# Three of four pooling groups by a seven-product scheme, with block sums made by adding DMAs

## The chip, the cores and the metric

One core of one Trainium2 chip runs the whole program as one launch. The metric is the device time of that launch in microseconds (us). TensorE is PE, VectorE is DVE, ScalarE is ACT, GpSimd is POOL, and SyncE is SP, which issues most DMAs.

## The reference, cut to what matters

Two layers run over 512 latent and 256 context tokens of width 1024. The first has four mLSTM heads beside four pooling groups. The second is windowed attention and is not touched. For a pooling group, with 256 channels, the reference computes two projections of the normalized stream h (768 tokens by 1024 features), the value u and the gate g, and then

```python
ug = u.astype(f32).reshape(bsz, n, P_GROUPS, P_GROUP_DIM)          # P_WINDOWS = (2, 4, 8, 16)
...
mean = win_sum / (hi - lo).astype(f32)[None, :, :, None]
mixed = jnp.einsum('bngc,gcd->bngd', mean - ug, pool_w.astype(f32))
return mixed.reshape(bsz, n, P_WIDTH) * pool_scale                 # then times silu(gate), then w_out
```

## The kernel before

Every fp32 product is made of three passes with high and low halves: weights and stream are split into a high half (cast on ACT) and a low half (subtraction on DVE, some on POOL), and PE adds high by high, high by low and low by high in PSUM.

The stream is kept transposed as hhi and hlo, eight tiles each of 128 features by 768 tokens. `dense_units` (L229) walks the list `chunks0` (L207) and yields the matmuls of the projections; a chunk is one projection of 256 channels, its weights come in four tiles of 256 KB. In the heads these matmuls fill the gaps of the recurrence; `side_work` puts pieces of other work between them (products of the time embedding on DVE, tiles `mjk`, L719). The chunk u of one pooling group already runs as filler in the last head; its matmuls (`acc_u`) and those of the transposes `ytp` (L918) end the head.

Then comes the pool stage. For a group, u and g are two halves m of 128 channels; a half is 48 matmuls, in turn with 512 and 256 columns (L260), three passes over eight feature tiles. `evict_u` (L949) copies the half from PSUM on ACT into a padded row `up`, adds windows on DVE (L961), multiplies by a table of reciprocal counts and subtracts (L964, L965), and splits the result into dh and dl. `evict_g` (L973) takes tanh on ACT and multiplies on DVE (L976). `mix` (L981) multiplies dh and dl by the group's 256 x 256 weights, 12 matmuls for a half, scales on DVE (L992) and stores the half (L993) into `ysp`. The mix of a group runs in the middle of the next group's u. PSUM accumulators of these projections come from `pacc` (L175), which has two buffers: a third must wait until the first is evicted.

The output projection (`po`, L1090) takes 16 such stored blocks with their weights `ows`; its first blocks are loaded ahead, behind marks of the pool stage (`MARK`, `MARKD`, L1073), and split on ACT (`owh`, `oyh`) and DVE (`owl`, `oyl`).

A Tile scheduler turns the text into one instruction queue for each engine, in program order, with semaphores; each engine takes its queue in order. POOL computes the scale of each head (`rs_hd`, `rr_hd`, L148, L150), which DVE needs at the end of that head (L909), and little else there.

Of the kernel before, what the change touches and what calls it, by code (L numbers as in the profile page):

```python
# [10 lines left out]
F32 = mybir.dt.float32  # L11
# [60 lines left out]
MARK = (3, 0)  # L72
# [7 lines left out]
MARKD = (2, 0)  # L80
SN = (1, 1, 1, 1)
SK = 3.0
# [25 lines left out]
def tile_trunk(ctx: ExitStack, tc: tile.TileContext, x, c, ctx_in, c_ctx, w_mod, b_mod, g_pre, g_post,  # L108
               w_in, b_gate, conv_w, mnorm, pool_w, pool_scale, w_out, c_w_in, c_sink, c_w_out,
               w_mod_t, w_mod_0, win_c, cwin_c, vecs, inv_cnt, cos_t, sin_t, out):  # L110
# [48 lines left out]
    ps2 = cst.tile([P, KT], F32, name="ps2")  # L159
    kcw = cst.tile([P, 48], F32, name="kcw")  # L160
# [49 lines left out]
    chunks0 += [(k_, g) for g in range(4) for k_ in "ug"]  # L210
# [88 lines left out]
    with ExitStack() as st0:  # L299
# [163 lines left out]
        V.tensor_scalar(ps2, cv[:, CPS:CPS + KT], 0.5, None, op0=ALU.mult)  # L463
        V.tensor_copy(kcw, cv[:, CCV:CCV + 48])
# [81 lines left out]
    ysp = [dram.tile([P, T], F32, name=f"ysp{i}") for i in range(16)]  # L546

    with ExitStack() as sth:
# [178 lines left out]
        def gate_half(l, w, n, ops):  # L727
# [4 lines left out]
            def item(k):  # L732
                wst = mp.tile([P, 512], F32, tag="wmt", name=f"wmg{nm}{k}", bufs=WB)
                SY.dma_start(wst, w_mod[l][k * P:(k + 1) * P, cols])
                yield
                if k == 0:
                    acc.append(mp.tile([P, 512], F32, tag="macc", name="macc" + nm, bufs=1))
                    G.memset(acc[0], 0.0)
                    SY.dma_start(acc[0][0:1, :], b_mod[l:l + 1, cols])
                ko(V.scalar_tensor_tensor(acc[0], wst, cs[:, w, k:k + 1], acc[0], op0=ALU.mult, op1=ALU.add))  # L740
# [28 lines left out]
        for h in range(H):  # L769
# [101 lines left out]
            def side_n(i):  # L871
                for _ in range(SN[i]):
                    side_work()

# [32 lines left out]
            r2 = rstd_from(ssq, 4 * DH, NT, gp, "hd")  # L907
            for t in range(NT):
                V.scalar_tensor_tensor(hs[:, t, :], hs[:, t, :], r2[:, t:t + 1], zz[:, t, :],  # L909
                                       op0=ALU.mult, op1=ALU.mult)  # L910
# [12 lines left out]
        while side or begun:  # L923
            side_work()


    with ExitStack() as stp:
        pp = stp.enter_context(tc.tile_pool(name="pool", bufs=2, reuse_waits="tile"))
        ups = []
        W_P = PAD + NX + PAD + NC + PAD  # L930
        WU = NX + PAD + NC
        for i in range(2):
            up = pp.tile([P, W_P], F32, name=f"up{i}", bufs=1)
            G.memset(up, 0.0)
            ups.append(up)

        cst_g, dd, zg = {}, {}, {}

        def pool_consts(g):
            ivt = pp.tile([P, WU], F32, tag="ivt", name=f"ivt{g}", bufs=1)  # L940
            SY.dma_start(ivt, inv_cnt[g:g + 1, :].to_broadcast([P, WU]))
            pws = pp.tile([P, 2, DH], F32, tag="pws", name=f"pws{g}", bufs=1)
            SY.dma_start(pws, pool_w[0, g].rearrange("(k p) c -> p k c", p=P))
            pwh = pp.tile([P, 2, DH], F32R, tag="pwh", name=f"pwh{g}")
# [655 lines left out]
```

## Time and profile before

| what | us |
|---|---|
| device time, median of 3 runs | 1094.92 (1093.55 to 1096.0) |
| device time of the profiled execution | 1093.02 |
| its span | 1091.1 |
| PE busy in the span | 1062.9 (97%) |
| DVE busy | 741.6 (68%) |
| ACT busy | 529.0 (48%) |
| POOL busy | 116.9 (11%) |

The time of a run is a little more than the span that the profiler shows, because the span begins and ends with the first and last instruction of an engine. Busy shares are of the whole span; what a stage is bound by is read from that stage.

### The profile page before, as it was taken

To read this page: it belongs to the slowest core of one execution; us is meant where nothing else is said; L and a number is where in the kernel's file an instruction comes from. 1 tells how busy PE (TensorE), PEld (TensorE's weight loads), DVE (VectorE), ACT (ScalarE), POOL (GpSimd) and SP (SyncE) were. 2 spreads that over 40 slices of the span, in tenths; PEclk is the share of its full clock that TensorE was granted. 3 is DMA by queue.
4 is the path that set the end of the run, shared out by engine and by line. 5 is a ranking of instruction groups with operands and counts; after the bars stand their busy time and mean duration, and the time that the engine had idled before them with its cause. 6 is when DMAs were issued, how large, how long until landed. Compare 5 with 4: busy or idle time off the path is not lost.

```text
span 1091.1 us, 18584 instructions
## 1 busy us (share of the span) xinstructions
PE 1062.9 (97%) x7071; PEld 959.4 (88%) x7071; DVE 741.6 (68%) x1638; ACT 529.0 (48%) x1025; POOL 116.9 (11%) x154
## 2 busy tenths in 40 slices
PE   8999999999999999999999999999999999999997
PEld 4898999999989998998888888878899999998875
DVE  4975775767677767778656455576574777777776
ACT  5953533344344433533232225465474666667772
POOL 2100000000000000001000000110015223214211
PEclk9999999999999999999999999999999999999999
DMA  8543352435333434334332348766213111103103
GB/s 341 166 146 88 102 142 73 140 107 134 95 121 114 119 101 132 101 103 126 112 117 82 111 140 276 231 209 237 72 40 90 57 40 57 50 21 97 40 20 116
DMA packets 66881, 127.26 MB, mean 117 GB/s; under 512 B 9884, under 2 KB 21340, under 8 KB 66792
## 3 DMA queue, kind: packets, MB, share of 16 engines
q1 hardware_dynamic: 66792, 126.08, 36.7%
q8 instruction: 55, 0.90, 0.3%
q14 instruction: 34, 0.28, 0.1%
HBM read 115.53 MB, written 10.52 MB: 116 GB/s over the span
## 4 chain that ended last, share of the span: by engine, by line
PE 84%; DVE 6%; issue 3%; ACT 3%; DMA 2%; POOL 1%; DVEq 0%; SPq 0%; POOLq 0%; ACTq 0%
PE po L1090 10%; PE acc_v L254 6%; PE acc_g L260 6%; PE acc_u L260 6%; PE acc_z L254 6%; PE acc_k L260 6%; PE acc_o L254 5%; PE acc_q L260 5%; PE acc1z L1368 4%; PE acc1q L1368 4%; PE ph L865 4%; PE pq L817 3%; PE pv L1300 2%; PE S L1262 2%; PE pt L1290 2%
## 5 line engine op out<-in xcount | busy, mean ns | idle before, releaser
L1090 PE MATMUL po<-owh,oyh 128*128 128x512 f32 x192 | 59.6, 391 | 1.2 <-DVE ytp L992 1.2
L1090 PE MATMUL po<-owl,oyh 128*128 128x512 f32 x192 | 59.7, 392 | 0.9 <-DVE owl L141 0.9
L136 ACT CAST ph<-pt 128x512 fp32r<-128x512 f32 x72 | 41.9, 584 | 36.5 <-PE pt L1290 35.9
L1090 PE MATMUL po<-owh,oyl 128*128 128x512 f32 x192 | 59.2, 389 | 0.0
L1277 ACT ACTIVATE p<-p,mx 128x512 f32<-128x512 f32 (+1 forms) x64 | 49.9, 780 | 12.7 <-DVE mx L1275 11.6
L254 PE MATMUL acc_v<-whi_v,hhi 128*128 128x256 f32 (+1 forms) x192 | 55.9, 291 | 0.0
L254 PE MATMUL acc_z<-whi_z,hhi 128*128 128x256 f32 x192 | 55.5, 289 | 0.0
L254 PE MATMUL acc_o<-whi_o,hhi 128*128 128x256 f32 x192 | 54.9, 286 | 0.0
L141 DVE TENSOR_TENSOR pl<-pt,ph 128x512 fp32r<-128x512 f32 x72 | 49.4, 688 | 7.5 <-ACT ph L136 7.0
L254 PE MATMUL acc_v<-whi_v,hlo 128*128 128x256 f32 (+1 forms) x192 | 54.3, 283 | 0.0
L254 PE MATMUL acc_v<-wlo_v,hhi 128*128 128x256 f32 (+1 forms) x192 | 54.2, 282 | 0.0
L254 PE MATMUL acc_z<-whi_z,hlo 128*128 128x256 f32 x192 | 53.9, 281 | 0.0
L254 PE MATMUL acc_o<-whi_o,hlo 128*128 128x256 f32 x192 | 53.8, 280 | 0.0
L254 PE MATMUL acc_o<-wlo_o,hhi 128*128 128x256 f32 x192 | 53.8, 280 | 0.0
L254 PE MATMUL acc_z<-wlo_z,hhi 128*128 128x256 f32 x192 | 53.7, 280 | 0.0
L141 DVE TENSOR_TENSOR owl<-ows,owh 128x1024 fp32r<-128x1024 f32 x32 | 39.1, 1222 | 14.0 <-ACT owh L136 14.0
L1411 PE MATMUL fin<-woh,ohl 128*128 128x512 f32 x128 | 47.7, 413 | 0.7 <-DVE ya L1418 0.7
L1273 DVE CUSTOM_DVE_ANT_0 p<-S,mA,nsk 128x512 f32<-128x512 f32 x48 | 35.9, 747 | 16.3 <-PE S L1262 15.8
L1090 PEld LDWEIGHTS po<-owl,oyh 128*128 128x128 f32 x192 | 35.7, 188 | 9.9 <-DVE owl L141 2.7
L719 DVE SCALAR_TENSOR_TENSOR mjk<-wmt,csb 128x512 f32<-128x512 f32 x64 | 43.7, 684 | 0.3
L1090 PEld LDWEIGHTS po<-owh,oyh 128*128 128x128 f32 x192 | 35.7, 188 | 8.8 <-issue 1.5
L1290 PE MATMUL pt<-ident,p 128*128 128x128 f32 x288 | 43.3, 273 | 0.1
(388 smaller groups left out, 3542.5 us busy)
## 6 DMA issues: line engine op xcount, KB each, us to landing
ows<-in_ab_w_out_dram SPq DMA_DIRECT2D x32, 512.0 KB, 5.4
wmg<-in_w_mod_dram SPq DMA_DIRECT2D x48, 256.0 KB, 2.7
wmod<-in_w_mod_dram SPq DMA_DIRECT2D x16, 512.0 KB, 6.7
wmt<-in_w_mod_t_dram SPq DMA_DIRECT2D x32, 256.0 KB, 3.2
oys<-ysp SPq DMA_DIRECT2D x32, 192.0 KB, 3.1
ws_q<-in_win_c_dram SPq DMA_DIRECT2D x16, 256.0 KB, 2.6
ws_v<-in_win_c_dram SPq DMA_DIRECT2D x16, 256.0 KB
ws_k<-in_win_c_dram SPq DMA_DIRECT2D x16, 256.0 KB, 2.6
```

The source lines that it names most:

```text
L136: S.copy(hi, src)
L141: (lo_eng or V).tensor_tensor(lo, src, f32(hi), op=ALU.subtract)
L254: ko(PE.matmul(acc[:, j, 0:cols], hx[k][:, ts_], ww[k // 2][:, k % 2, 0:cols], start=(k == 0 and i == 0), stop=(k == KT - 1 and i == 2)))
L260: ko(PE.matmul(acc[:, a:b], ww[k // 2][:, k % 2, sl], hx[k][:, a:b], start=(k == 0 and i == 0), stop=(k == KT - 1 and i == 2)))
L719: ko(V.scalar_tensor_tensor(jk, wst, 1.0, csb[:, w_, hf * 512:hf * 512 + 512], op0=ALU.mult, op1=ALU.mult, accum_out=md[:, which, kt, hf, ...
L865: ko(PE.matmul(ph[:, 0:DH], ss[:, s, :], vv[:, s, :], start=(j == 0 and i == 0), stop=(j == len(stl) - 1 and i == 2)))
L1090: ko(PE.matmul(accs[j][:, ns], yy[:, j * P:(j + 1) * P], ww[:, ns], start=(k == 0 and i == 0), stop=(k == 15 and i == 2)))
L1273: V.tensor_tensor_reduce(p_[:, 0:512], pS, mask[:, 0:512], -0.125, sk, ALU.add, ALU.min, mx)
L1277: S.activation(p_[:, 0:n], p_[:, 0:n], AF.Exp, scale=-1.0, bias=mx, accum_out=self.den[:, hh:hh + 1])
L1290: ko(PE.transpose(tp[:, hh * P:(hh + 1) * P], self.ps[hh][:, j * P:(j + 1) * P], ident))
L1368: ko(PE.matmul(acc[:, j, :], hx[t0 + j][:, k, :], ww[k // 2][:, k % 2, :], start=(k == 0 and i == 0), stop=(k == KT - 1 and i == 2)))
L1411: ko(PE.matmul(acc, ohl[:, x_, k, :], ww[4 * b + k][:, ns], start=(k == 0 and pi == 0), stop=(k == 3 and pi == 2)))
```

## The change

Group 1 is computed as before, u in the last head and g first in the pool stage. Groups 3, 2 and 0 are computed by Strassen's scheme in Winograd's form: for a group, u and g (two halves of output channels), two halves of the 1024 features and two halves of the 768 tokens make a 2 x 2 by 2 x 2 block product, which takes seven block products of 256 channels by 512 features by 384 tokens in place of eight. A block product is 24 matmuls, 12 for each half m of 128 channels (four feature tiles, three passes), with 384 columns each (L1144). Three accumulators (y and x from `pacc`, z from `pmisc`) hold partial results that ACT copies out between products and DVE adds.

The scheme needs sums of blocks of h and of the weights. Those of the weights (12 tiles of 512 KB in DRAM) are made by a plain DMA and an adding DMA, both on POOL's queue (`keep_w`, `add_w`). The stream is first put together from its halves in DRAM, in the same way (`keep_h`, `add_h`). That is 40 DMAs of 384 or 512 KB; `sum_step` issues up to 12 in each head. At the end of the last head four blocks of the stream (`raw`, 768 KB each) are loaded back, added and subtracted on DVE (`diff`), cast on ACT (`high`), and the low halves are made on DVE (one) and POOL (three) (`low`).

The windows run over both halves of a group at once (2 x 791 elements), and the reciprocal counts are applied at the edges only. The mixes of one group are put into the products of the next. The first block of the output projection has its own buffers, loaded early; the second waits for the marks.

```diff
+    def keep_h(k):
+        ko(G.dma_start(hdr[k], f32(hhi[k])))
+    def add_h(k):
+        ko(G.dma_start(hdr[k], f32(hlo[k]), accum_op=ALU.add))
+    def keep_w(key, src):
+        ko(G.dma_start(wsum[key], src))
+    def add_w(key, src):
+        ko(G.dma_start(wsum[key], src, accum_op=ALU.add, max_dma_last_dim=8192))
...
             def side_n(i):
...
+                if i != 1 and n < 4:
+                    sum_step()
...
+        raws = {n: hs_p.tile([P, 4, TH], F32, tag="sum", name=f"raw{n}", bufs=5) for n in "6752"}
+        for n, (kk, tt) in zip("7562", ((0, 0), (0, 1), (1, 1), (1, 0))):
+            SY.dma_start(raws[n], hdr[4 * kk:4 * kk + 4, :, TH * tt:TH * tt + TH].rearrange("k p t -> p k t"))
...
+        def high(n):
+            highs[n] = hi_p.tile([P, 4, TH], F32R, name=f"high{n}")
+            with tc.issue_after(zg["u"]):
+                S.copy(highs[n], raws[n])
+        def low(n):
+            lows[n] = hs_p.tile([P, 4, TH], F32R, tag="sum", name=f"low{n}", bufs=5)
+            (G if n in "752" else V).tensor_tensor(lows[n], raws[n], f32(highs[n]), op=ALU.subtract)
...
-        def mix(g):
+        def mix(g, m):
...
+            if g == PAIRS[-1]:
...
+                S.copy(mixed, acc[:, 0:T])
+                acc = mixed
...
+        USES = "1265743"
+        def product(acc, g, n, start, ms=(0, 1)):
+            x_ = operand(n)
+            for m in ms:
+                for k in range(4):
+                    if k == 1:
+                        load_w()
+                    if k == 3:
+                        step()
+                    hi, lo = ready_w[g, n, k // 2]
+                    xh, xl = x_(k)
+                    for i, (ww, hx) in enumerate(((hi, xh), (hi, xl), (lo, xh))):
+                        ko(PE.matmul(acc[:, m, 0:TH], ww[:, k % 2, m * P:(m + 1) * P], hx, ...
+        def pair(g, before):
+            y, z = two(new_acc(f"y{g}")), two(pmisc.tile([P, 1024], F32, tag="qk", name=f"z{g}"))
+            product(y, g, "1", True)
+            ko(S.copy(p1, y[:, :, 0:TH]))
+            product(z, g, "2", True)
+            ko(V.tensor_tensor(up[:, :, PAD:PAD + TH], z[:, :, 0:TH], p1, op=ALU.add))
+            product(y, g, "6", False)
...
+            product(x_, g, "5", True, (0,))
+            product(y, g, "7", False)
...
+            mix(before, 0)
+            product(y, g, "4", False)
...
+            product(x_, g, "5", True, (1,))
...
+            mix(before, 1)
+            product(x_, g, "3", False)
...
+            b = V.tensor_tensor(gx[:, :, L], x_[:, :, 0:TH], gx[:, :, L], op=ALU.add)
+            if last:
+                marks["b"] = b.ins
...
+                    if gi == 0 and k == 0:
+                        ws, ys = first
```

The change moves instructions at places that the diff does not show. The first is DVE where the pool stage opens, from the windows of the first group to the gate's first half `zg`, whose instruction sets an accumulator free (`raw`, `win`, `df`, `dl` are rows of the pool stage, `pwl` and `wlo` low halves of weights). Before, the last head's scale `hs3` stands ahead of it; then:

```order
L961 TENSOR_TENSOR win000_6161<-up0_6147 128x791
L964 TENSOR_TENSOR df00_6163<-win000_6161,ivt0_6151 128x776
L965 TENSOR_TENSOR df00_6163<-df00_6163,up0_6147 128x776
L141 TENSOR_TENSOR pwl0_6156<-pws0_6153,pwh0_6155 128x512
L961 TENSOR_TENSOR win010_6172<-up1_6149 128x791
L141 TENSOR_TENSOR dl00_6167<-df00_6163,dh00_6166 128x776
L964 TENSOR_TENSOR df01_6174<-win010_6172,ivt0_6151 128x776
L965 TENSOR_TENSOR df01_6174<-df01_6174,up1_6149 128x776
L141 TENSOR_TENSOR pwl1_6333<-pws1_6330,pwh1_6332 128x512
L141 TENSOR_TENSOR dl01_6178<-df01_6174,dh01_6177 128x776
L976 SCALAR_TENSOR_TENSOR zg00_6242<-zg00_6242,acc_g00_6193 128x768
```

In the changed kernel the same stretch, behind the four `raw` instructions, reads

```order
L140 TENSOR_TENSOR wlo_311_6341<-ws_311_6339,whi_311_6340 128x2x256
L1043 TENSOR_TENSOR win10_6351<-up_6228 128x2x791
L1031 TENSOR_TENSOR low6_6329<-raw6_6216,high6_6327 128x1536
L140 TENSOR_TENSOR pwl1_6368<-pws1_6226,pwh1_6367 128x512
L1043 TENSOR_TENSOR win11_6401<-win10_6351 128x2x789
L1048 TENSOR_TENSOR win11_6401<-win11_6401,ivt1_6224 128x2x8
L1048 TENSOR_TENSOR win11_6401<-win11_6401,ivt1_6224 128x2x24
L1048 TENSOR_TENSOR win11_6401<-win11_6401,ivt1_6224 128x2x8
L1050 SCALAR_TENSOR_TENSOR win11_6401<-win11_6401,up_6228 128x2x776
L140 TENSOR_TENSOR pwl3_6378<-pws3_6375,pwh3_6377 128x512
L1074 SCALAR_TENSOR_TENSOR zg1_6285<-zg1_6285,acc_g10_6234 128x768
```

The windows of both halves and the edges now stand ahead of the first gate half in longer instructions, with the low half of one block of the stream between them.

The second is DVE a little ahead of it, at the end of the last head (`hs3` is the head's output, `ot3` its squares, `wlo_g` a low half of a gate weight). Before:

```order
L903 SCALAR_TENSOR_TENSOR hs3_5180<-ot3_5349,hs3_5180 128x1536
L905 SCALAR_TENSOR_TENSOR ot3_5349,ssqh_1151<-hs3_5180 128x256 x6
L909 SCALAR_TENSOR_TENSOR hs3_5180<-hs3_5180,rr_hd_5990,zt3_5766 128x256 x6
L141 TENSOR_TENSOR wlo_g02_6038<-ws_g02_6036,whi_g02_6037 128x2x256
L141 TENSOR_TENSOR wlo_g03_6056<-ws_g03_6054,whi_g03_6055 128x2x256
```

and now:

```order
L946 SCALAR_TENSOR_TENSOR hs3_5252<-ot3_5427,hs3_5252 128x1536
L948 SCALAR_TENSOR_TENSOR ot3_5427,ssqh_1166<-hs3_5252 128x256 x6
L140 TENSOR_TENSOR wlo_g12_6114<-ws_g12_6112,whi_g12_6113 128x2x256
L140 TENSOR_TENSOR wlo_g13_6132<-ws_g13_6130,whi_g13_6131 128x2x256
L955 SCALAR_TENSOR_TENSOR hs3_5252<-hs3_5252,rr_hd3_6066,zt3_5839 128x256 x6
```

Two weight halves that stood behind the scaling of `hs3` by `rr_hd` now stand ahead of it.

The third is POOL, from the end of the heads to the first work behind the pool stage. Before:

```order
L738 MEMSET macc101_5439 128x512
L148 TENSOR_SCALAR rs_hd_5988<-ssqh_1151 128x6
L150 TENSOR_TENSOR rr_hd_5990<-rs_hd_5988,mhalf_67 128x6
L934 MEMSET up0_6147 128x792
L934 MEMSET up1_6149 128x792
L141 TENSOR_TENSOR wlo_q00_8549<-ws_q00_8547,whi_q00_8548 128x512
```

and now:

```order
L568 DMA wsum02_750<-wsum05_749 16x8192
L571 DMA wsum02_750<-in_win_c_dram 64x2048
L568 DMA wsum04_751<-wsum02_750 16x8192
L571 DMA wsum04_751<-in_win_c_dram 64x2048
L951 TENSOR_SCALAR rs_hd3_6064<-ssqh_1166 128x6
L953 TENSOR_TENSOR rr_hd3_6066<-rs_hd3_6064,mhalf_67 128x6
L1010 MEMSET up_6228 128x1584
L1031 TENSOR_TENSOR low7_6448<-raw7_6217,high7_6331 128x1536
L1031 TENSOR_TENSOR low5_6470<-raw5_6218,high5_6468 128x1536
L1031 TENSOR_TENSOR low2_6493<-raw2_6219,high2_6491 128x1536
```

The last four DMAs of the block sums stand in head 3, and three low halves of the stream (1536 elements for each partition) come in where POOL had nothing to do.

The fourth is ACT at the start of the output projection (`owh`, `oyh` are its operands, `whi_k` a later weight). Before:

```order
L136 CAST oyh00_7333<-oys00_7329 128x384
L136 CAST owh00_7331<-ows00_7327 128x1024
L136 CAST oyh01_7363<-oys01_7359 128x384
L136 CAST owh01_7361<-ows01_7357 128x1024
L975 ACTIVATE zg31_7242<-acc_g31_7193 128x768
L136 CAST whi_k0_8063<-ws_k0_8062 128x512
L136 CAST whi_k1_8069<-ws_k1_8068 128x512
```

and now:

```order
L1057 CAST dh0_7334<-win00_7284 128x1552
L135 CAST oyh00_7430<-oys00_6203 128x384
L135 CAST owh00_7428<-ows00_6202 128x1024
L1201 ACTIVATE zg0_7339<-gx0_7044 128x1536
L1093 COPY mixed_7355<-acc_mix00_7342 128x768
L135 CAST whi_k0_8160<-ws_k0_8159 128x512
L135 CAST owh01_7458<-ows01_7454 128x1024
L1093 COPY mixed_7355<-acc_mix01_7359 128x768
L135 CAST oyh01_7460<-oys01_7456 128x384
```

The copy of the last mix's second half stands behind the cast `owh01`, whose load waits for the marks.

## Rows read from the trace of the kernel before

**Rows 1.** The page: busy time of the engines over the span (busy us, share, instructions).

```profile
PE 1062.9 (97%) x7071; PEld 959.4 (88%) x7071; DVE 741.6 (68%) x1638; ACT 529.0 (48%) x1025; POOL 116.9 (11%) x154
```

**Rows 2.** Stretches of the span with the busy time of each engine in them (us from the start of the span; busy us and number of instructions for each engine, then the granted TensorE clock, the share of the DMA engines and GB/s). The four are the end of the gates with the first head's opening, the rest of the first head, the pool stage, and the first 30 us of the output projection.

```profile
100.00:125.00 25.00, 22.82 (x188) 22.25 (x187) 16.29 (x50) 13.36 (x31) 0.00 (x0) 1.00 0.34 99
125.00:235.00 110.00, 110.00 (x811) 103.87 (x810) 78.76 (x198) 45.45 (x90) 2.97 (x4) 1.00 0.39 117
514.00:650.00 136.00, 134.85 (x768) 117.62 (x768) 81.13 (x105) 38.17 (x63) 0.00 (x0) 1.00 0.35 112
650.00:680.00 30.00, 29.72 (x130) 24.36 (x131) 15.56 (x20) 12.80 (x19) 0.25 (x1) 1.00 0.83 273
```

**Rows 3.** The chain of work that ended last, through the pool stage (start us, length us, what; x is the number of matmuls). Pieces left out repeat the pattern with the other groups.

```profile
512.27 0.61 ACT whi_u L136
...
513.73 0.28 ACT up L952
...
514.06 17.08 PE acc_g L260 x96
531.14 8.40 PE acc_u L260 x48
539.54 4.20 PE acc_mix L988 x24
...
644.64 4.28 PE acc_mix L988 x24
...
648.95 1.03 DVE ytp L992
...
650.11 12.51 PE po L1090 x54
```

**Rows 4.** The same chain in a head: a run of matmuls with 256 columns each.

```profile
118.30 4.25 PE acc_o L254 x36
```

**Rows 5.** The same chain in the output projection: a run of matmuls with 512 columns each.

```profile
752.16 16.39 PE po L1090 x72
```

**Rows 6.** DVE instruction by instruction at the end of the last head (start us, length us, instruction, in brackets the idle time before it and what ended it).

```profile
505.08 2.46 DVE L909 SCALAR_TENSOR_TENSOR hs<-hs,rr_hd,zt 128x256 f32<-128x256 f32 x6 [2.15 <-POOL rr_hd L150]
507.47 1.28 DVE L141 TENSOR_TENSOR wlo_g<-ws_g,whi_g 128x512 fp32r<-128x512 f32 x2
508.67 0.68 DVE L719 SCALAR_TENSOR_TENSOR mjk<-wmt,csb 128x512 f32<-128x512 f32 x1
...
509.39 0.69 DVE L719 SCALAR_TENSOR_TENSOR mjk<-wmt,csb 128x512 f32<-128x512 f32 x1
```

**Rows 7.** ACT at the same place.

```profile
506.65 0.62 ACT L136 CAST whi_g<-ws_g 128x512 fp32r<-128x512 f32 x1 [1.49 <-PE acc_u L260]
```

**Rows 8.** Groups of DVE instructions by form over the whole run (busy us, mean ns of one, idle time of DVE before them). From the top: 768 elements with one operand in PSUM, 1536 elements with both in SBUF.

```profile
L976 DVE SCALAR_TENSOR_TENSOR zg<-zg,acc_g 128x768 f32<-128x768 f32 x8 | 7.6, 953 | 8.2 <-ACT zg L975 8.1
...
L903 DVE SCALAR_TENSOR_TENSOR hs<-ot,hs 128x1536 f32<-128x1536 f32 x4 | 7.0, 1757 | 8.8 <-ACT hs L867 8.8
```

**Rows 9.** Groups of POOL instructions by form over the whole run, same columns.

```profile
L141 POOL TENSOR_TENSOR wol<-wos,woh 128x512 fp32r<-128x512 f32 x16 | 20.8, 1316 | 23.8 <-issue 14.0 <-ACT woh L136 9.9
L1321 POOL TENSOR_TENSOR og<-gt,ot 128x256 f32<-128x256 f32 x12 | 8.9, 738 | 54.4 <-DVE ot L1320 44.0 <-ACT p L1277 10.3
```

**Rows 10.** POOL instruction by instruction at one place of the output projection.

```profile
679.75 2.56 POOL L141 TENSOR_TENSOR wlo_q<-ws_q,whi_q 128x512 fp32r<-128x512 f32 x2 [173.30 <-ACT whi_q L136]
...
685.22 1.30 POOL L141 TENSOR_TENSOR wlo_q<-ws_q,whi_q 128x512 fp32r<-128x512 f32 x1 [0.22 <-ACT whi_q L136]
```

**Rows 11.** DVE there.

```profile
676.34 0.55 DVE L141 TENSOR_TENSOR oyl<-oys,oyh 128x384 fp32r<-128x384 f32 x1
...
681.32 1.40 DVE L141 TENSOR_TENSOR oyl<-oys,oyh 128x384 fp32r<-128x384 f32 x1 [1.82 <-ACT oyh L136]
...
685.59 1.35 DVE L141 TENSOR_TENSOR oyl<-oys,oyh 128x384 fp32r<-128x384 f32 x1 [1.74 <-ACT oyh L136]
```

**Rows 12.** POOL instruction by instruction at one place near the end of the run.

```profile
1053.84 1.28 POOL L141 TENSOR_TENSOR wol<-wos,woh 128x512 fp32r<-128x512 f32 x1 [2.12 <-ACT woh L136]
```

**Rows 13.** DVE there.

```profile
1053.90 1.25 DVE L1282 TENSOR_TENSOR es<-mx,snk 128x4 f32<-128x4 f32 x1
```

**Rows 14.** One tile of DVE over the whole run: duration ns min/median/max.

```profile
L1282 DVE TENSOR_TENSOR es<-mx,snk x16: 149/156/1246, 846.2 to 1053.9; 128x4 f32<-128x4 f32 x16
```

**Rows 15.** The chain of work in the first head's opening.

```profile
98.93 9.46 DMA qb<-qdr
...
109.32 0.84 ACT kh L136
...
110.19 0.97 DVE kl L141
...
111.20 0.50 PE pq L817 x2
```

**Rows 16.** POOL's instructions in the heads.

```profile
82.09 0.22 POOL L631 COPY pad<-lf 128x48 f32<-128x48 f32 x1 [2.10 <-DVE lf L629]
...
178.22 0.58 POOL L148 TENSOR_SCALAR rs_hd<-ssqh 128x6 f32<-128x6 f32 x1 [18.72 <-DVE ot L905]
...
288.76 0.51 POOL L148 TENSOR_SCALAR rs_hd<-ssqh 128x6 f32<-128x6 f32 x1 [5.45 <-DVE ot L905]
```

**Rows 17.** DMA issues, from the page and from the stretch 630 to 660 us: KB each, median us from issue to landing.

```profile
ows<-in_ab_w_out_dram SPq DMA_DIRECT2D x32, 512.0 KB, 5.4
...
wmod<-in_w_mod_dram SPq DMA_DIRECT2D x16, 512.0 KB, 6.7
...
ysp<-ytp SPq DMA_DIRECT2D x2, 384.0 KB, 2.3
```

**Rows 18.** DVE in the first head, 125 to 235 us: the groups of tensor_scalar.

```profile
L838 DVE TENSOR_SCALAR eb<-ef,rd 128x128 f32<-128x128 f32 (+2 forms) x4 | 1.3, 337 | 0.1
...
L166 DVE TENSOR_SCALAR A<-md,b,cv 128x2 f32<-128x2 f32 x2 | 0.6, 284 | 0.0
```

**Rows 19.** ACT, a group over the whole run: the cast of an output-projection weight.

```profile
L136 ACT CAST owh<-ows 128x1024 fp32r<-128x1024 f32 x32 | 33.6, 1051 | 5.0 <-DMA ows<-in_ab_w_out_dram 5.0
```

More of the change, by code (lines that the diff above doesn't have):

```diff
@@ L922, in tile_trunk @@
                 upto("k", h + 1, side_work)
[L923 to L924 removed]
+        with tc.issue_after(tail["v"]):
+            while side or begun:
+                side_work()
+        while sums:
+            sum_step()
+    ops = ExitStack()
+    op0 = ops.enter_context(tc.tile_pool(name="op0", bufs=1, side="right", reuse_waits="tile"))
+    first = op0.tile([P, D], F32, name="ows00"), op0.tile([P, 384], F32, name="oys00")
     with ExitStack() as stp:
[L928 removed]
@@ L997, in tile_trunk @@
-        pool_consts(0)
-        evict0.update(u=evict_u, g=evict_g)
-        for g in range(4):
-            upto("g", g)
-            if g < 3:
-                pool_consts(g + 1)
-        mix(3)
+            else:
+                acc = pmisc.tile([P, 1024], F32, tag="qk", name=f"mix{g}{m}")
+            for k in range(2):
+                for i, (ww, dx) in enumerate(((pwh, 0), (pwh, 1), (pwl, 0))):
+                    for a, e_, o_ in ((0, NX, 0), (NX, T, PAD)):
+                        ko(PE.matmul(acc[:, a:e_], ww[:, k, m * P:(m + 1) * P], dd[g][dx][:, k, a + o_:e_ + o_],
+                                     start=(k == 0 and i == 0), stop=(k == 1 and i == 2)))
@@ new lines, in tile_trunk, with opening @@
+        evict0.update(u=evict_u, g=evict_g)
+        def opening():
+            for n in "7562":
+                diff(n)
+                yield
+            high("6")
+            low("6")
+            high("7")
+            yield
+            yield from win_steps(FIRST_G)
+            low("7")
+            yield
+            for n in "52":
+                high(n)
+                low(n)
+                yield
+        todo.append(opening())
+        n = 0
+        while ("g", FIRST_G) not in done0:
+            if next(stream0, None) is None:
+                break
+            n += 1
+            if n > 4 and n % 2:
+                step()
+            if n >= SWN and n % 2 == 0:
+                load_w()
@@ L1004, in tile_trunk @@
+        list(consts)
+        SY.dma_start(first[0], w_out[0, 0:P, :])
+        SY.dma_start(first[1], ysp[0][:, 0:384])
+        list(pool_consts(PAIRS[0]))
+        prior = FIRST_G
+        for g in PAIRS:
+            pair(g, prior)
+            prior = g
+        while todo:
+            step()
+        mix(prior, 0)
+        mix(prior, 1)
     l0.close()
```

241 lines of the change are left out of this document (182 added, 59 removed).

## The prediction

> **What bounds the kernel now.** The busy times come first: PE works 97% of the span [rows 1]. The stretches show where: PE is busy 134.85 of 136 us in the pool stage and all of 110 us in a head, at a granted clock of 1.00, while DVE has 55 us to spare in the one and 31 in the other [rows 2]. The chain of waits then names what ends each piece of the pool stage: runs of matmuls one behind the other, and two short breaks, 1.8 us while ACT copies the last u (512.27 to 514.06) and 1.2 us before the output projection [rows 3]. So a matmul saved in the pool stage is worth its whole time, as long as the other engines keep up.
>
> **What the products save.** A group's u and g are 192 matmuls. Runs of 96 and 48 of them take 16.82 and 8.40 us [rows 3], 175 ns each, so 33.6 us a group. The seven products are 168 matmuls with 384 columns, which no row shows. A run of 36 with 256 columns takes 4.25 us [rows 4], 118 ns each, and 72 with 512 columns 16.39 us [rows 5], 228 ns. Halfway is 173 ns; the alternation of both kinds in u and g gives 175. With 173 to 175 a group costs 29.0 to 29.4 us. The saving is 4.2 to 4.6 us a group, over three groups 12.6 to 13.8. I take **-13.2**. The mixes stay 24 matmuls a group, 4.2 us [rows 3].
>
> **The opening of the pool stage** is the largest cost. PE's first product needs an accumulator, and both are held by the gate of group 1 until DVE has done the first `zg`. By the order, that instruction stands behind everything that prepares the sums and the windows.
>
> I add up DVE from the end of the head. Before, the scaling of `hs` ran from 505.08 to 507.5, with two weight halves behind it [rows 6]. Now these stand ahead, and the second waits for its cast, which ended at 507.27 [rows 7]. With 0.64 for that half and 2.46 for `hs`, DVE is free at 510.4, 2.9 us later than before. Then come four `mjk` at a spacing of 0.72 (508.67 to 509.39) [rows 6], 2.9; four `raw` of 1536 elements at 1.76 [rows 8], 7.0; two weight halves 1.3 and small pieces 0.6; the first window, 1582 elements, 1.8; the low half of a block, 1.76. This is 525.8. Two `pwl`, a window, three edges and the difference add 5.4, and `zg` itself 0.95 [rows 8]: 532.1. PE asks for the accumulator at 514.06 + 16.82 = 530.9 [rows 3]. So far 1.2 us late.
>
> But from 525.8 on POOL makes three low halves of 1536 elements. POOL took 0.738 us for 256 and 1.316 for 512 [rows 9], so 3.6 us each by extension, 10.8 in all. And the trace shows what DVE does beside such work. An `oyl` of 0.55 us took 1.40 when it came at 681.32, in the middle of POOL's subtractions, and 1.35 at 685.59, where POOL's ran until 686.52 [rows 10, 11]. At 1053.90 an addition of four elements took 1.25 us and ended just when POOL's instruction of 1.28 us did [rows 12, 13]; its median is 156 ns [rows 14]. All these have both operands in SBUF, and so have the two `pwl`, the window, the edges and the difference.
>
> The bounds are these. If a POOL instruction holds DVE only for as long as a row shows, 1.3 us, three of them cost 3.9 and the first product is 5.1 late. If each holds it to its own end, it is 12.0 late. The rows are nearest to the second, since each hold ended with POOL's instruction; but DVE gets a turn between two, and the durations added up overlap by some 0.07 us each. I take **+8.5**; nothing at all is possible only if POOL comes later than DVE's whole row.
>
> The Trainium skill, "SBUF — State Buffer", section "Who interferes with whom", says that a DVE instruction with two SBUF inputs contends with a GpSimd instruction that reads SBUF, and that the one that comes second blocks fully until the other is done. By that rule the term is the upper bound, 12.0, and my sum comes out 3.5 us longer; the trace agrees for instructions of up to 1.3 us, and none here is longer.
>
> **Smaller terms.** The later `hs` also feeds PE's transposes at the head's end; PE has 48 matmuls of u to put between. Between 0 and the 2.9 us above, I take **+0.8**.
>
> The 12 DMAs that POOL issues from 82 us on [rows 16] meet the load of `qb`, 768 KB, which took 9.46 us and ends a wait of PE (98.93 to 111.20) [rows 15]; that stretch has 2.2 us of PE idle in 25 [rows 2]. Shared between two queues the load could take twice as long, +9.5, or be untouched. The adding DMAs come one after the other, each behind its plain one, so they leave gaps: **+0.6**.
>
> Between the pairs, each has 14 weight tiles to split where a group had 8; 18 more at 0.64 are 12 us of DVE [rows 6], and the opening's 9 us come on top. DVE's 81 us in the stage [rows 2] become some 105 of 123, so a late split now and then: 0 to 3, I take **+0.8**. The load itself rises from 112 GB/s to below 200, where 273 have been moved [rows 2].
>
> The output projection started 1.2 us after the last mix, behind `ytp` of 1.03 us [rows 3]. Now PE's first `po` waits for ACT's copy of the last half mix, which by the order stands behind the cast `owh01`. That weight is loaded only when the last addition on DVE is done, some 1.3 us after the last product. The load takes between 2.3 and 5.4 us by the rows for 384 and 512 KB [rows 17], the cast 1.05 [rows 19] and the copy about 0.8: PE starts 5.5 to 8.6 us after the last product, with 4.2 us of mix in between, so after a break of 1.3 to 4.4 instead of 1.2. I take **+2.0**.
>
> At nothing I cost the windows of the later pairs and the sums in DRAM of the later heads: DVE's spare time and the 61% of the DMA engines' time that is free in a head [rows 2] cover them. If that cover goes, the scaling of the next head's output is late (second rival).
>
> Sum: -13.2 + 8.5 + 0.8 + 0.6 + 0.8 + 2.0 = **-0.5 us**. Against the profiled execution's 1093.02 that is 1092.5; the runs' median is 1.9 higher, 1094.92, which gives **1094.4**.
>
> **The rivals.** *The opening keeps up.* POOL's low halves fall behind DVE's row, or DVE takes its turns first; the stall is 0 to 3 us and PE keeps the saving: 1094.9 - 13.2 + 1.5 + 4.2 = 1087.4, or 1081.7 when the small terms and the stall vanish. For it: the low halves are needed only some 12 us into the pair, and POOL's start hangs on ACT's casts. Against it: each hold in rows 10 to 14. Chance 0.27.
>
> *The blocks of the stream come late* (slower). Four loads of 768 KB in pieces of 1.5 KB must land before DVE can begin; the last is wanted at about 520. If SP issues them at about 500 (an estimate from where the head's tiles come free, rows 6), 273 GB/s [rows 2] lands 3.1 MB in 11.5 us, but the rate of `qb` [rows 15] needs 38. From below some 150 GB/s on, every microsecond later is one of PE: up to 17 more, 1111. Chance 0.09.
>
> *POOL's DMAs are slow* (slower). POOL takes its queue in order, and `rs_hd` of head 0 stands behind 12 of them. From 82.1 to 178.2 [rows 16] there are 96 us, 8.0 for each. The rows for 384 to 512 KB, 2.3 to 6.7 [rows 17], fit; 9.46 would not, and cost 17 us in head 0 and 5 in the next (288.76 less 180.2 is 108.6), 1117. Chance 0.07. The Trainium skill, "SBUF — State Buffer", section "SBUF: two separate sides", warns that a DMA issued from GpSimd waits for its descriptors while DVE runs an instruction in a two-port mode; copies, casts and tensor_scalar are of that kind. In a head of 110 us DVE has 1.9 us of tensor_scalar [rows 18], so by that rule the rival gains nothing.
>
> *The matmul with 384 columns costs as much as two with 256.* Then 168 cost 236 ns each and the saving turns into a loss of 18 us; even at 190 ns it shrinks to 5. Rows 4 and 5 speak for a straight line. Chance 0.05.
>
> **How the numbers follow.** The forecast has 0.47, its own range is 1089 to 1100; the rest, 0.05, lies close to no change. A measurement of this kernel tells about 0.2%, 2.2 us, from no change, so faster is below 1092.7 and slower above 1097.1. The forecast is spread over 0.14 faster, 0.20 same, 0.13 slower; the first rival adds 0.27 to faster, the three others 0.21 to slower, the rest 0.05 to same. Faster 0.41, same 0.25, slower 0.34. The range, 1084.5 to 1104, leaves out the best of the first rival and most of the two slow ones.
>
> **What would show it.** Right: a run of 24 product matmuls takes 4.1 to 4.2 us; POOL's three low halves stand one by one beside stretched DVE instructions after 520 us; PE stands still for 5 to 12 us before the first product, released by DVE `zg`; the break before `po` is 2 to 4 us, released by ACT. Wrong: no gap over 3 us before the first product (first rival); `raw` on DVE waiting for a DMA (second); `rs_hd` later than 180 us behind POOL's DMAs (third); products slower than 180 ns a matmul (fourth).

## The result, and the profile after

The changed kernel takes 1110.78 us (1109.25 to 1112.49, 4 runs) beside 1095.46 for the kernel before (1093.55 to 1096.98, 4 runs): a ratio of 1.0139, 95% interval 1.0121 to 1.0158, slower by 1.4%. The forecast was 1094.4 with a range of 1084.5 to 1104. The profiled execution took 1109.25 with a span of 1107.6, so 16.5 us more span than before.

First its busy times and its DMA queues, from the page.

```profile
PE 1059.4 (96%) x6999; PEld 963.2 (87%) x6999; DVE 770.4 (70%) x1660; ACT 552.2 (50%) x1051; POOL 156.0 (14%) x190
...
q1 hardware_dynamic: 71496, 132.43, 38.4%
q0 software_dynamic: 3136, 18.88, 7.7%
```

PE is busy 3.5 us less than in [rows 1] and stands still for 20 us more. POOL's 40 transfers are the queue q0.

Where the time went is read by following one point of the program: the last pair of `ytp` transposes of the heads, and the first `acc_g` of the pool stage (start, length, what; after).

```profile
527.51 0.38 PE L964 MATMUL ytp<-ident,hs 128*128 128x128 f32 x2
529.21 0.62 PE L260 MATMUL acc_g<-hhi,whi_g 128*128 128x512 f32 x2 [1.31 <-ACT up L1069]
```

Before, the same:

```profile
512.10 0.38 PE L918 MATMUL ytp<-ident,hs 128*128 128x128 f32 x2
```

The heads end 15.4 us later, and the first `acc_g` starts 15.2 later. From there to the first `po` the pool stage takes 133.5 us (529.21 to 662.68) where it took 136.0 [rows 3]: 2.6 less. In the output projection the same instructions fall 2.8 us further behind, in the rest of the run 1.1. That is 15.2 - 2.6 + 2.8 + 1.1, the 16.5: **the loss is in the heads, where nothing was computed differently**. POOL's `rr_hd` gives it by head:

```profile
186.30 1.37 POOL L953 TENSOR_TENSOR rr_hd<-rs_hd,mhalf 128x6 f32<-128x6 f32 x1
...
298.36 1.67 POOL L953 TENSOR_TENSOR rr_hd<-rs_hd,mhalf 128x6 f32<-128x6 f32 x1
...
411.84 1.68 POOL L953 TENSOR_TENSOR rr_hd<-rs_hd,mhalf 128x6 f32<-128x6 f32 x1
...
517.23 1.35 POOL L953 TENSOR_TENSOR rr_hd<-rs_hd,mhalf 128x6 f32<-128x6 f32 x1
```

Before, these stood at 178.88, 289.35, 399.18 and 503.72: late by 7.4, 9.0, 12.7 and 13.5 us. Next, stretches of the changed kernel (busy us of each engine, then granted clock, DMA share, GB/s): the first head's opening, two heads, the wait of the pool stage, its products.

```profile
108.00:113.00 5.00, 0.70 (x6) 0.49 (x5) 2.67 (x7) 1.96 (x5) 1.42 (x2) 1.00 0.91 259
113.00:120.00 7.00, 6.27 (x27) 5.98 (x28) 3.93 (x14) 2.00 (x6) 1.44 (x2) 0.52 0.69 140
125.00:235.00 110.00, 108.22 (x787) 101.13 (x786) 78.29 (x197) 44.10 (x87) 9.34 (x13) 1.00 0.60 167
235.00:345.00 110.00, 108.13 (x786) 100.86 (x785) 77.83 (x202) 42.62 (x85) 10.05 (x14) 1.00 0.61 169
...
545.00:564.00 19.00, 11.31 (x57) 10.90 (x56) 15.42 (x12) 6.82 (x10) 7.44 (x2) 0.82 0.29 82
564.00:662.00 98.00, 96.90 (x553) 94.11 (x551) 69.20 (x80) 44.31 (x67) 0.00 (x0) 1.00 0.44 134
```

From 108 to 113 the DMA engines are 91% busy and PE nearly stands still; then it has half its clock for 6.8 us (1.2 GHz in place of 2.4). Before, these 12 us held 9.82 us of PE's work at 1.00. In a head PE loses 1 to 2 us of 110, where [rows 2] had none. The waits of PE (us in total, times, longest) and the time to landing of some transfers (KB each, median us):

```profile
PE acc_y L1144 <- DVE zg L1074: 7.7, 1, 7.7
PE pq L858 <- ACT kh L135: 4.6, 1, 4.6
PE stp L895 <- DVE sl L140: 2.8, 4, 1.0
PE po L1340 <- DVE owl L140: 2.7, 5, 0.8
```

```profile
wsum<-in_win_c_dram POOLq DMA_DIRECT2D x18, 512.0 KB, 6.6
...
hdr<-hhi POOLq DMA_DIRECT2D x8, 384.0 KB, 5.1
hdr<-hlo POOLq DMA_DIRECT2D x8, 384.0 KB, 4.8
...
ysp<-yt SPq DMA_DIRECT2D x8, 384.0 KB, 5.2
```

The first line of the waits is the predicted one. PE's wait for `kh` was 1.6 us before. The store `ysp`, which the change does not touch, took 2.3 us before. Its buffers are the value convolution's, so ACT's `cv_q` waits for it (before, then after):

```profile
ACT cv_q L555 <- DMA ysp<-yt: 2.8, 1, 2.8
```

```profile
ACT cv_q L596 <- DMA ysp<-yt: 15.0, 3, 5.6
```

DVE, which waits for `cv_q`, did so for 16.0 us before and does for 25.7 now.

The opening of the pool stage, POOL and then DVE beside it (start, length):

```profile
538.50 14.02 POOL L1031 TENSOR_TENSOR low<-raw,high 128x1536 fp32r<-128x1536 f32 x3 [12.71 <-DVE low L1031]
```

```profile
540.70 3.57 DVE L1048 TENSOR_TENSOR win<-win,ivt 128x16 f32<-128x16 f32 x3
544.31 4.92 DVE L1050 SCALAR_TENSOR_TENSOR win<-win,up 128x1552 f32<-128x1552 f32 x1
549.16 3.91 DVE L140 TENSOR_TENSOR pwl<-pws,pwh 128x512 fp32r<-128x512 f32 x1
553.00 0.94 DVE L1074 SCALAR_TENSOR_TENSOR zg<-zg,acc_g 128x768 f32<-128x768 f32 x1
```

The three edges have 16, 48 and 16 elements; the first alone took 3.37 of their 3.57 us. `zg` comes right behind the third held instruction. POOL's three instructions took 5.54, 3.49 and 4.84 us.

### The profile page after: what moved, and what is told of

Same layout as the page of the kernel before. It is cut to its first block, busy times and chain, and to the rows that moved or that the text cites. A ratio compares the mean times of both kernels' runs of the same rounds, so it can differ in the third digit from the quotient of the medians.

```text
span 1107.6 us, 18618 instructions
## 1 busy us (share of the span) xinstructions
PE 1059.4 (96%) x6999; PEld 963.2 (87%) x6999; DVE 770.4 (70%) x1660; ACT 552.2 (50%) x1051; POOL 156.0 (14%) x190
## 4 chain that ended last, share of the span: by engine, by line
PE 34%; DVE 7%; issue 3%; DMA 3%; ACT 3%; POOL 1%; DVEq 0%; POOLq 0%; ACTq 0%; SPq 0%
PE po L1340 8%; PE acc_y L1144 4%; PE acc1q L1619 4%; PE acc1z L1619 3%; PE pv L1551 2%; PE S L1513 2%; PE pt L1541 2%; PE acc1v L1398 2%; PE acc1k L1398 2%; PE acc_x L1144 2%; PE z L1144 1%; PE fin L1662 1%; PE mix L1086 1%; DVE pl L140 1%; DMA ows<-in_ab_w_out_dram 1%
## 5 line engine op out<-in xcount | busy, mean ns | idle before, releaser
L140 DVE TENSOR_TENSOR owl<-ows,owh 128x1024 fp32r<-128x1024 f32 x32 | 39.4, 1230 | 15.3 <-ACT owh L135 15.2
L135 ACT CAST whi<-ws 128x512 fp32r<-128x512 f32 x42 | 25.8, 620 | 42.9 <-DMA ws<-wsum 18.7
L140 DVE TENSOR_TENSOR wlo<-ws,whi 128x512 fp32r<-128x512 f32 x42 | 28.4, 687 | 26.4 <-ACT whi L135 25.0
L140 POOL TENSOR_TENSOR wlo_q<-ws_q,whi_q 128x512 fp32r<-128x512 f32 x16 | 21.7, 1359 | 172.7 <-DMA oys<-ysp 145.5
```

What stands on the lines that cost most here:

```text
L135: S.copy(hi, src)
L140: (lo_eng or V).tensor_tensor(lo, src, f32(hi), op=ALU.subtract)
```

## The experiments

All are edits of the changed kernel, unless said otherwise; "e" numbers are in the order of the runs. The kernel before, run beside each, had medians from 1094.8 to 1096.1. A profile shows one execution, and which one matters here: that of e4 is the fastest of its ten, those of e6 and e9 are the slowest of four and seven.

**e1 and e8: without the sums, and with those of the stream alone.** e1 empties the list and loads other blocks; e8 keeps the list's first sixteen entries.

```diff
+    sums.clear()                      # e8: del sums[16:]
...
-    SY.dma_start(raws[n], hdr[4 * kk:4 * kk + 4, ...])
+    SY.dma_start(raws[n], win_c[4 * kk + tt, 0:4, :, 0:TH]...)    # e1 only
...
-    n, lambda: wsum[g, {"6": "2", "7": "3"}.get(n, n)])()[i]
+    n, lambda: block(g, 1, 0))()[i]
```

> The changed kernel without its 40 block-sum DMAs; the blocks and the weights are loaded from other places of the same size, so the values are not the reference's. Theory A (the sums collide with the DMAs of the heads): PE reaches the last u's end about where the kernel before does, some 15 us earlier than in the changed kernel, no half clock near 113 us; 1094 to 1098 us. Theory B (the heads lose to side work that moved, and to memsets that DVE now does, the sums are hidden): within 3 us of the changed kernel's 1110.8.

> The changed kernel with the sums of the stream only, 16 DMAs in head 0 and at the start of head 1; the weight sums are left out and the weights loaded from other places, so the values are not the reference's. If every DMA costs alike, 24 of 40 parts of 15 us come back: 1101 to 1103. If it is the wait for the query rows and the half clock behind it that count, most of the loss stays: 1103 to 1107. If the DMAs from DRAM to DRAM are the dear ones: 1096 to 1100.

e1: 1095.04, ratio 0.9993 (0.9978 to 1.0009). e8: 1102.03, ratio 1.0046 (1.0027 to 1.0064). So the sums cost 15.7 us by the medians, 7.0 for those of the stream and 8.7 for those of the weights; by the ratios it is 16.0, 5.8 and 10.2, each with some 2.7 us either way. In the heads PE, ACT and SP take the same instructions in the same order in e1 and in the changed kernel. DVE's order differs at the ends of three heads; the only wait of PE that shows there, `ytp` on `hs`, is 0.5 us. Within that error e8 fits its first theory, that every transfer costs alike. In e1 the heads are full again, and `ysp` lands in 2.3 us. But the clock falls at the first head's opening in e1 too, for a shorter time (third line):

```profile
125.00:235.00 110.00, 110.00 (x809) 103.67 (x808) 79.93 (x203) 45.52 (x91) 1.91 (x2) 1.00 0.39 117
235.00:345.00 110.00, 110.00 (x815) 104.27 (x815) 80.75 (x206) 45.36 (x91) 1.84 (x2) 1.00 0.42 118
...
113.00:120.00 7.00, 7.00 (x53) 7.00 (x53) 3.95 (x14) 4.02 (x9) 0.00 (x0) 0.85 0.14 37
```

**e4 and e5: the three low halves on DVE, with the sums and without.**

```diff
-            (G if n in "752" else V).tensor_tensor(lows[n], ...)
+            V.tensor_tensor(lows[n], ...)
```

> The changed kernel with the three low halves of the stream's blocks on DVE instead of POOL. Theory A2 (POOL's instructions hold DVE at the opening): the stall before the first product falls from 7.7 us to 3 or less and the half clock after it goes, 6 to 10 us come back: 1101 to 1105. Rival (DVE simply has too much to do there): its row grows by up to 5.3 us, the stall to 11 or 13: 1113 to 1117.

> Both at once: no block-sum DMAs (the blocks and weights are loaded from other places of the same size, so the values are not the reference's) and the three low halves on DVE. Theory: the sums and the hold at the opening are all that eats the saving of the products, so 6 to 10 us come off the kernel without sums (1095.0): 1085 to 1089, 0.7 to 1.0% faster than before. Rival: a third cost of some size is left, in the pairs or before the output projection: 1091 to 1095.

e4: 1104.16, ratio 1.0061 (1.0042 to 1.008). e5: 1087.83, ratio 0.9918 (0.9895 to 0.994). The same edit gives 6.6 and 7.2 us by the medians, 8.5 and 8.2 by the ratios. In e4 the held instructions are short:

```profile
541.60 0.37 DVE L1048 TENSOR_TENSOR win<-win,ivt 128x16 f32<-128x16 f32 x3
...
543.56 1.77 DVE L1050 SCALAR_TENSOR_TENSOR win<-win,up 128x1552 f32<-128x1552 f32 x1
```

Against 3.57, 4.92, and 3.91 (`pwl`, here 0.69), each hold was 3.2 us. PE waits 2.3 us for `zg` in place of 7.7, and the clock does not fall there.

**e6: 44 matmuls that nobody reads, ahead of the first product.** They tell whether half the clock comes from PE's standing still.

```diff
+        fill = pmisc.tile([P, 1024], F32, tag="qk", name="fill")
+        for _ in range(44):
+            ko(PE.matmul(fill[:, 0:TH], hhi[0][:, 0:P], hhi[0][:, 0:TH], start=True, stop=True))
```

> The changed kernel with 44 idle matmuls of 384 columns put ahead of the first product, where PE stands still for 7.7 us; their result is read by nobody. They fill the wait without shortening it. If the half clock after the wait comes from PE's standing still, it goes, and 3 to 5 us come back: 1106 to 1108. If the clock falls for another reason, or costs nothing, 1110 to 1112.

1108.08 (1104.35 to 1113.11), ratio 1.0109 (1.0069 to 1.0148). With PE busy the clock stays:

```profile
550.00:557.00 7.00, 7.00 (x42) 6.86 (x41) 7.00 (x2) 2.64 (x4) 6.92 (x2) 1.00 0.02 3
```

The gain is not told apart from the scatter of these four runs; in the changed kernel PE waits through more than half of the time at half the clock there, and the nine matmuls that it does at that clock take 3.0 us where 1.6 would do.

**e2 and e7: the kernel before with the 40 transfers, which nobody reads** (in e7 with the memset of `macc` on DVE, as the changed kernel has it).

```diff
+                if i != 1 and n < 4:
+                    sum_step()
...
+        while sums:                      # at the end of the heads
+            sum_step()
...
-                    G.memset(acc[0], 0.0)        # e7
+                    V.memset(acc[0], 0.0)
```

> The kernel before, with the same 40 DMAs added at the same places of POOL's queue, and nothing that reads their sums. Theory A: 10 to 15 us slower than before, 1105 to 1111, with the wait for the query rows and a half clock near 113 us. Theory B: 1095 to 1098.

> The kernel before with the 40 DMAs added and, as in the change, the memsets of macc on DVE instead of POOL's queue. Theory A (the 40 DMAs cost the heads 15 us): 1108 to 1113. The 65 us of the run with the DMAs alone are then the memsets of macc and the scales of the heads, which stood in POOL's queue between DMAs that wait. Rival (the DMAs themselves cost 65 us there, and the change hides most of it): 1140 to 1162.

1161.14 and 1158.62, ratios 1.0589 (1.0565 to 1.0613) and 1.0574 (1.0533 to 1.0616): both expectations fell. They do not price the sums either. Nobody reads the transfers, so nothing sets when they must be done: in e7 nine of the forty stand behind 531 us, and the order of other work moves. The waits of PE in e7:

```profile
PE acc_g L260 <- ACT up L994: 19.9, 1, 19.9
PE h1t L1093 <- ACT jk L1084: 16.3, 2, 14.1
PE acc_k L260 <- DVE cv_q L597: 10.7, 3, 7.8
```

The first comes about on ACT: the copy `up` now stands behind two casts of the pool weights, of which the first waits 13.24 us for its load `pws` while the DMA engines are 0.90 busy (545 to 558). Before, `up` stood ahead of them. The second comes behind a cast that waits 6.9 us for a load of `ws_q`. What they show is what a late load costs where an engine that takes its work in order has other work behind it.

**e3: the sums spread out**, up to three in a step, each group behind a tiny POOL operation that reads `hs`.

```diff
-                if i != 1 and n < 4:
+                if i != 1 and 0 < n < 5 and sums:
+                    if i == 0:
+                        pc = gp.tile([P, 1], F32, tag="pace", ...)
+                        ko(G.tensor_scalar(pc, hs[:, order[n - 1], 0:1], 1.0, 0.0, ...))
                     sum_step()
```

> The changed kernel with the sums paced: from the second step of a head's six on, three a step, each group of three behind a tiny POOL instruction that reads the output of the step before. Theory A: the query rows' load and the stores at a head's start are alone again, so 6 to 12 us come back: 1099 to 1105, no half clock near 113 us. Theory B: no change, 1109 to 1112. If it is the bytes and not the place that counts, only the first wait goes: 1104 to 1106.

1140.04, ratio 1.0401 (1.0363 to 1.0438): 29 us worse than the bursts, and outside everything that was expected. `ysp` lands in 2.3 us again, but `ws_q` in 12.6 and `qb` in 10.1. The largest wait of PE is

```profile
PE ytp L967 <- DVE hs L958: 14.9, 3, 6.2
```

and it comes from a moved order, not from a late load. In the changed kernel `hs` stands ahead of the next head's weight splits (293.65 and 297.52); here it stands behind them:

```profile
296.43 1.40 DVE L140 TENSOR_TENSOR wlo_q<-ws_q,whi_q 128x512 fp32r<-128x512 f32 x2 [4.64 <-ACT whi_q L135]
...
301.14 1.75 DVE L949 SCALAR_TENSOR_TENSOR hs<-ot,hs 128x1536 f32<-128x1536 f32 x1
```

The cast `whi_q` that the split waits for had itself waited for PE's `acc_v`, as it does in the changed kernel. The same happens at the ends of the next two heads. So e3 does not tell what spreading the transfers does by itself.

**e9 and e10: the low halves on DVE, and the sums elsewhere.** e9 starts the first burst behind the first value copy; e10 also moves the last group's eight sums to the start of the pool stage, ahead of the pairs (not behind the first groups' products, as its expectation says).

```diff
-                if i != 1 and n < 4:
+                if i != 1 and (n < 4 if h else 0 < n < 5):       # with e3's tiny operation ahead, once
...
+        for what, *args in late:                                  # e10, ahead of the pairs
+            what(*args)
```

> The changed kernel with the three low halves on DVE, and the first head's twelve sums not ahead of its first query block but behind its first value copy (one tiny POOL operation that reads that copy stands ahead of them). Against the same kernel with the low halves on DVE alone (1104.2). Theory A, the sums of the opening cost by where they land, beside the loads of the first query block and the first weight: the half-clock stretch near 113 us goes, the first value waits under 3 us, and the time falls by 4 to 7, to 1097 to 1100. Theory B, the sums cost by the bytes they move, wherever they are: within 1.5 us of 1104.2. Theory C, pushed later they meet the next head's loads: 1106 or more, with a wait for cv_q.

> The run before it (late first burst, low halves on DVE), and the last group's eight weight sums taken out of the heads and put behind the pool stage's products of the first groups, where POOL stands idle and its weights are wanted last. Theory A (the sums cost because their bursts meet the heads' loads and stores): 8 of 40 fewer there give back 2 to 4 us, 1093 to 1097. Theory B (bytes): no change against the run before it. Theory C (the weights come late for the last group): PE waits for its casts late in the pool stage, and the time is 2 us or more above the run before it.

e9: 1100.22 (1096.01 to 1105.97), ratio 1.0052 (1.0032 to 1.0073). What follows is its slowest execution. The stretch at 113 is at full clock, and PE works 9.5 of these 12 us again:

```profile
108.00:113.00 5.00, 2.50 (x19) 2.09 (x18) 3.12 (x10) 1.95 (x5) 0.00 (x0) 1.00 0.19 68
113.00:120.00 7.00, 7.00 (x62) 7.00 (x61) 5.37 (x22) 4.40 (x10) 0.51 (x2) 1.00 0.13 40
```

But now DVE's memset of `macc` waits 7.63 us for a small store of the tile to land, `sl` stands behind it, PE waits 4.7 us for `sl`, and half the clock follows at 169:

```profile
167.81 0.48 DVE L778 MEMSET macc<- 128x512 f32 x1 [7.63 <-DMA ggd<-macc]
...
168.36 0.54 DVE L140 TENSOR_TENSOR sl<-stp,sh 128x384 fp32r<-128x384 f32 x1
```

That memset was POOL's before the change. In the changed kernel it does not wait at this place. Against e4's ratio the gain of e9 is not told apart from nothing. e10: 1114.33, ratio 1.0169 (1.0146 to 1.0193), the third theory. There the transfers meet `pws`, whose casts hold ACT and, behind it, the gate, and late in the stage a cast that waits 10.6 us for its load `ws` costs PE a second wait of 6.7 us:

```profile
544.48 0.62 ACT L135 CAST pwh<-pws 128x512 fp32r<-128x512 f32 x1 [4.46 <-DMA pws<-in_ab_pool_w_dram]
```

**e11 to e14: is it the bytes, the adding, or the number?** e11 copies where the change adds; e12 and e13 move 16 of 128 partitions and load the sums from one row; e14 does both.

```diff
-        ko(G.dma_start(hdr[k], f32(hlo[k]), accum_op=ALU.add))
+        ko(G.dma_start(hdr[k], f32(hlo[k])))                      # e11
+        ko(G.dma_start(hdr[k], f32(hlo[k][0:16]), accum_op=ALU.add))   # e12, e13 (e14 without accum_op)
```

> The changed kernel with its twenty adding transfers made plain copies of the same size, from the same queue and at the same places; so the sums are not formed (the second block overwrites the first). Theory A, what costs is the traffic of forty transfers beside the heads' own loads: the time stays within 3 us of the changed kernel, 1108 to 1113. Theory B, the adding itself is dear (it lands later and holds the engines of the DMA longer than a copy): half or more of the 15.7 us that the sums cost goes, 1095 to 1103.

> The changed kernel with the same forty transfers at the same places, each moving only the first 16 of 128 partitions (48 or 64 KB in place of 384 or 512); the blocks of the stream and the weights that are sums are then loaded from one row of these for all partitions, as many bytes as before, the four stream blocks in sixteen pieces. The products get wrong data. Theory A, what costs is the bytes in the same stretch: an eighth of 15.7 us is left, 1096 to 1099. Theory B, what costs is the number of transfers, their issue on POOL or the order that waits behind them: 1105 to 1111, as the changed kernel.

> The run with an eighth of the bytes again, but each block of the stream loaded by one transfer, not four: SP took 13.8 us to issue twelve of the sixteen pieces there, the next weights stood behind them, and PE waited 9.6 us for ACT's copy `up` before its first `acc_g`. Theory A, those pieces made that wait and most of what the sums cost are bytes: the wait for `up` is under 2 us, the first `acc_g` starts at 518 to 523 us of the span (516 without sums, 529 with all their bytes), 1097 to 1102. Theory B, the number of transfers, whatever they move: first `acc_g` after 525, 1105 or more.

> The run before it with plain copies in place of the twenty adding transfers (an eighth of the bytes, nothing added). With it the four cases stand side by side: all bytes or an eighth, added or copied. If adding costs by its bytes, this run is within 1.5 us of the one before; if each adding transfer costs by itself, whatever its size, it is 2 to 5 us faster, 1095 to 1098.

1103.99, 1107.03, 1108.28 and 1106.58; ratios 1.0075 (1.0058 to 1.0092), 1.0101 (1.0084 to 1.0117), 1.0118 (1.0097 to 1.0139) and 1.0096 (1.0077 to 1.0116). The times of the last three are no price of the sums. They have a wait of their own, PE's for `up` ahead of `acc_g` (9.6, 8.7 and 9.8 us), and my reason for it, the sixteen pieces, fell with e13: one transfer for each block waits the same. That the reads of one row for all partitions make it is not shown; e13 has the DMA engines full at 190 GB/s among them, where the changed kernel moved 287 at 0.87 in the same 8 us.

```profile
516.00:524.00 8.00, 6.99 (x45) 6.04 (x43) 5.91 (x11) 3.01 (x5) 1.42 (x1) 1.00 1.02 190
```

e11 has no such wait, and its time is a price: without the adding 6.8 us come back (7.0 by the ratio), and 9.0 stay. That lies between its two theories. e13 and e14 are 1.7 us apart, within the scatter.

The heads come before that wait, so for the others I compare where the last `ytp` of the heads starts; e1 and e14:

```profile
514.24 0.38 PE L966 MATMUL ytp<-ident,hs 128*128 128x128 f32 x2
```

```profile
518.30 0.38 PE L964 MATMUL ytp<-ident,hs 128*128 128x128 f32 x2
```

| sums | start, us | later than e1 |
|---|---|---|
| none (e1, e5) | 514.24, 514.88 | 0, 0.6 |
| all bytes, added (after, e4, e6) | 527.51, 525.15, 532.53 | 13.3, 10.9, 18.3 |
| all bytes, copied (e11) | 523.93 | 9.7 |
| an eighth, added (e12, e13) | 519.66, 522.61 | 5.4, 8.4 |
| an eighth, copied (e14) | 518.30 | 4.1 |

These are single executions. The changed kernel, e4 and e6 have the same heads, instruction by instruction, and differ by 7.4 us; e12 and e13 by 3.0. So the table shows that the bytes count: each start with an eighth of them lies ahead of each with all. It does not resolve the adding, which is priced by the times of e11. Forty small copies still come out 4 us late, more than the two kernels without sums differ. So no single one of the three is the whole cause, and how the last 4 come about is open.

## Why the prediction was wrong

**The step that failed** is the one on the sums in DRAM, in its two sentences. "So they leave gaps: +0.6" took almost the lower of two bounds, 0 and 9.5, because the adding transfers follow one another. In four executions with these twelve transfers `rr_hd` of the first head comes 4.2, 5.1, 7.5 and 8.3 us later than in e1 (e4, the changed kernel, e8, e6). And "at nothing I cost ... the sums in DRAM of the later heads" named 61% of free DMA time as their cover. With all forty the later heads add 6.7, 8.1 and 10.0 us (e4, the changed kernel, e6). e1 measured 15.7 for both together.

What showed in place of the step: with one transfer of 384 or 512 KB after another the DMA engines are 0.91 busy from 108 to 113 and 0.99 from 206 to 222, and a load or a store that is due there lands late: `qb` of the first head is used at 109.2 (106.1 before, 107.3 in e1), `ysp` took 5.2 us. Engines that take their work in order pass the delay on: `cv_q`, `sl`, `kh`, then PE. And where PE stands still in a head, half the clock can follow: 0.52 from 113 to 120, which costs some 3 us beside the 4.6 of the wait. The share of free time in [rows 2], a mean over 110 us, says nothing of that. e9 and e10 show the same from the other side: at both other places the transfers met another load or store that was due.

The other 2.1 of the 15.4 us are in e1 as well, and they are lost ahead of the first head's end, where e1's `rr_hd` is 2.3 us later than before. There PE waits 1.9 us for `kh` (1.6 before), and the clock is 0.85 from 113 to 120 where it was 1.00. The forecast had no term for it; why the clock falls there in e1 and not in the kernel before is not shown.

The Trainium skill, "DMA: Bandwidth & Descriptors", section "Latency and other measured facts", says that the access latency of the memory, which makes up most of a transfer's fixed cost, is 0.2 us on average and 2 us at high load. The runs agree in direction: `ysp` went from 2.3 to 5.2 us, and fell to 2.3 without the sums.

**The products, -13.2**, were right. A run of 24 takes 4.19 us, 175 ns each (173 to 175 forecast); the chain of the changed kernel:

```profile
564.01 4.19 PE acc_y L1144 x24
568.20 2.10 PE acc_x L1144 x12
570.29 4.23 PE acc_y L1144 x24
```

With sums and holds away e5 is faster than before by 0.8%. The pool stage, from `acc_g` to `po`, gained 2.6 us; the terms that lie in it, -13.2 + 8.5 + 0.8 + 2.0, make -1.9.

**The opening, +8.5**, was right in mechanism and nearly in size: 7.7 us of wait, released by `zg`; e4 brings it to 2.3. The size is partly luck, since two parts balance: the three holds took 3.2 us each, 9.6 in place of the 7.3 that 8.5 less 1.2 leaves for them, and DVE's own row was some 3 us shorter than I had added up. The half clock behind the wait, some 1.4 us, had no term. The 3.6 us for a low half were good: the one in the middle, with DVE held all through, took 3.49, and the other two are longer where DVE had its turn. The Trainium skill, "SBUF — State Buffer", section "Who interferes with whom", has the second of two such instructions blocked until the first is done. The trace agrees in that, for either engine; its result, 12.0, was too long, since DVE got a turn between two of POOL's, as I had assumed in going below it.

**Later `hs`, +0.8**: PE waits 0.5 us for it at the first `ytp`. **The start of `po`, +2.0**: the break is 1.6 us, not 3.2 (1.2 before). Behind it 2.8 us are lost that I had not costed, most of them in the waits for `owl`, 2.7 in place of 0.9. **Between the pairs, +0.8**: from 564 to 662 PE stands still for 1.1 us in all.

**The rivals.** The opening did not keep up. `raw` on DVE waited for no DMA. `rs_hd` was not held by POOL's transfers: POOL stood idle for 62.33 us ahead of it. That rival had the right cause, transfers at 5 to 8 us in a row, and the wrong victim: it looked along POOL's own queue, not at whose loads they slow. The matmul of 384 columns costs what the straight line gives.

No version that forms the sums beat the kernel before: the best, e9, has a ratio of 1.0052. The 1087.8 of e5 is what the scheme would be worth with its sums for nothing.

## What to carry to other kernels

A free share of DMA time is no cover. Before new traffic is costed at nothing, list which loads and stores fall due in the same microseconds and who waits in order behind them; where the bounds were 0 and 9.5, the first head alone lost 4 to 8 us. An intermediate that must pass through DRAM is to be paid like any other operation: here it took more than the saved matmuls gave (15.7 us against some 13). And before an experiment that moves transfers is read as their price, compare the order of the engines' queues: in e3 and e7 it had moved, and the moved order made the largest waits.

## What the runs showed of the hardware that was not expected

- A two-input subtraction of 1536 elements on POOL held a two-input DVE instruction behind it for 3.2 us each time, even an edge of 16 elements (3.37 us in place of 0.17). POOL waits in its turn: 3.49 us with DVE held all through, 4.84 and 5.54 where DVE had begun first.
- An adding transfer of 384 KB landed after 4.8 us, a copy in its place after 2.7; of 48 KB after 3.1 and 2.0 (e11, e13, e14).
- The granted clock fell to 0.5 for 6.8 us where PE had stood still for some microseconds, and stayed at 1.00 when matmuls that nobody reads filled the place ahead of the first product (e6).
- With loads of a block for 128 partitions from a single row the DMA engines were full at 190 GB/s for 8 us (e13).
